# Six tiles of split weights that begin at six different places of a 64 byte line, in a two-layer hybrid mixer block

## The chip, the cores and the metric

One core of a Trainium2 chip runs the whole program in one launch. The metric is the device time of that launch in microseconds (us). A core has five engines that run side by side: TensorE (PE in the profile, with its loads of weights as a row of their own, PEld), VectorE (DVE), ScalarE (ACT), GpSimd (POOL) and SyncE (SP), which issues the transfers from main memory.

## The reference

Two layers of a block that mixes four branches: retention with a decay in both directions, a short gated convolution of 3 taps, a convolution of 31 taps with a layer norm, and windowed attention with grouped keys. Each layer has a stream x of 512 tokens and a context stream of 256 tokens, both 1024 wide; in the second layer the context gives only keys, values and states.

```python
hx = modulate(rmsnorm(x, norm_w[l]), shift_x[:, None], scale_x[:, None])
px = split_proj(hx @ w_in[l])                 # 1024 -> 11008 columns
...
merged = sum(jax.nn.sigmoid(g) * (br @ w_branch[i]) for i, (g, br) in enumerate(...))
out = merged @ w_out
x = x + gate_x[:, None] * out_x
```

Everything is float32. What matters here is that nearly all of the arithmetic is `activations @ weights`, with weights that are used once per stream.

## The kernel before, in words

**Products.** Activations lie transposed, 128 features on the partitions and the tokens along a row: 512 columns for x, 256 for the context. A product runs in the type float32r, and to keep precision each operand is split in two parts, a high part (h) and a low part (l). `mm3` (L478) makes three matmuls for each of the eight blocks of 128 features: (weight h, x h), (weight h, x l), (weight l, x h). The weight block of 128x128 is what is loaded into the array, the activations stream through it, so every matmul comes with a load of its own and a tile of weights, 128x1024, gives 24 matmuls.

**Split weights.** A tile of raw weights comes by a transfer into one of two tiles `w0`, `w1` (or, while the context stream is worked on, into two rows of 512 columns). `w_split` (L445) then makes the two parts: ScalarE copies the raw weights into `wh` (which rounds them to float32r), VectorE subtracts that from the raw weights and writes `wl`. The parts go to the next of three pairs of tiles, `self.wt` (L292): wh0 and wl0, wh1 and wl1, wh2 and wl2, taken in turn by `take("wt")` (L448). `w_ahead` (L461) splits up to two tiles of weights ahead of the one in use, so ScalarE writes into a pair as soon as the matmuls of the tile three before it are done. The branch weights `w_b` (L450 to L454) and the activations are split into rows of another pool and don't use these six tiles.

**Other loads into the array.** The attention and retention products load blocks of rows; transposes load 128 columns of a row or of a probability tile `p`; the modulation (L559) loads four columns of a small tile `s4` at a time: `self.s4[:, 2 * h + k]` (L568), eight places that lie 16 bytes apart, against activations of 256 columns.

**Order.** TensorE's order is written by hand; side work (attention, retention, convolutions, norms) is woven between the matmuls of the projections by `slot` (L337), by estimates of when each engine is free. None of these estimates looks at an address. The order of the streams is context of layer 0, x of layer 0, keys and values of the context in layer 1, x of layer 1, and the last projection in two halves of 256 columns (L1267).

**Where tiles lie.** The pool `cp` (L290) lays its tiles one behind the other: `w0`, `w1`, the six tiles of split weights, six tiles `p` for attention, constants, vectors, and small tiles. A tile of 1024 float32 is 4096 bytes of each partition, 64 lines of 64 bytes.

**The convolution of 31 taps** (L878) is a row of VectorE instructions `y[a:b] += w * u[a+d:b+d]` with d from -15 to 15: for a negative d the write begins -d elements into its row, for a positive d the read begins d elements into its row.

Of the kernel before, what the change touches and what calls it, by code (L numbers as in the profile page):

```python
# [9 lines left out]
F32R = mybir.dt.float32r  # L10
# [15 lines left out]
P = 128  # L26
# [97 lines left out]
class Row:  # L124
# [3 lines left out]
    def __init__(self, free, ring, tile, w, parts):  # L128
        self.free, self.ring = free, ring
        self.r = tile[:, :w] if parts else None  # L130
        self.a = tile[:, :w].bitcast(F32) if parts else tile[:, :w]
# [146 lines left out]
class Block:  # L278
    def __init__(self, ctx, tc, xc, vec, cst, w_a, w_g, w_b, w_o, w_m, out):
        self.tc, self.nc = tc, Tally(tc.nc)  # L280
        self.xc, self.out = xc, out
        self.wsrc = {"a": w_a, "g": w_g, "b": w_b, "o": w_o}
        self.w_m = w_m

        rp = ctx.enter_context(tc.tile_pool(name="rp", bufs=1))
        rp.tile([P, PAD], F32, name="fill")
        self.arena = Arena(rp, NROWS, 12)
        self.arena.relief = self.relief

        self.cp = cp = ctx.enter_context(tc.tile_pool(name="cp", bufs=1))  # L290
        self.wraw = [cp.tile([P, 1024], F32, name=f"w{i}") for i in range(2)]
        self.wt = [[cp.tile([P, 1024], F32R, name=f"w{p}{i}") for p in "hl"] for i in range(3)]  # L292
        self.pt = [cp.tile([P, 640], F32, name=f"p{i}") for i in range(6)]
        pp = ctx.enter_context(tc.tile_pool(name="pp", bufs=1, space=PSUM))
        nc = self.nc
        self.cst = cp.tile([P, NC_], F32, name="cst")
        self.vec = cp.tile([P, NV], F32, name="vec")
        nc.sync.dma_start(self.vec, vec)
        nc.sync.dma_start(self.cst[:, :NCE], cst[:, :NCE])
        self.late_consts = lambda: nc.sync.dma_start(self.cst[:, NCE:], cst[:, NCE:])  # L300
        self.rings = {}
        self.dense = [pp.tile([P, 512], F32, name=f"d{i}") for i in range(3)]
        self.ovs = [pp.tile([P, 512], F32, name="ov")]
        self.work = [pp.tile([P, 512], F32, name=f"k{i}") for i in range(4)]
        self.turn = {}
        self.wq, self.wraws, self.wready, self.wkeep = [], [], {}, {}
        self.lanes = [[] for _ in range(5)]
        self.turns = 0
        self.flow = None
# [1161 lines left out]
```

## Time and profile before

| | us |
|---|---|
| median of 3 runs | 1832.24 (1830.57 to 1833.15) |
| the profiled execution, its own time | 1832.62 |
| its span, first to last instruction | 1830.5 |
| TensorE matmul busy in it | 1799.5 |
| VectorE busy | 1329.4 |
| ScalarE busy | 847.1 |

The span is shorter than the execution's own time by 2.1 us, which lies around the first and the last instruction. A matmul's bar in the trace is longer than its share of the time, because matmuls overlap: from one to the next only the distance of their starts counts. TensorE is busy in all but 31 us of the span, most of those at the start and at the end.

### The profile page before, as it was taken

The numbers are of one execution on the slowest core, as the hardware profiler recorded it, in microseconds if no ns is written. First come the engines' busy times: TensorE is split into PE (matmuls) and PEld (weight loads), VectorE is DVE, ScalarE is ACT, GpSimd is POOL, SyncE is SP. The second block draws the span as 40 slices with busy tenths as digits, with TensorE's granted clock in tenths as the row PEclk, the third lists the DMA queues.
The fourth block names the chain that finished last, engine by engine and source line by source line (L and its number), as shares of the span: only waits on it lengthen the run. The fifth ranks groups of instructions, "written<-read, shape, count | busy, mean of one in ns | idle before, by whom it ended". The sixth has DMA issues, their size and how long they took to land. (4 is left out here: it accounts for less than half of the span.)

```text
span 1830.5 us, 27546 instructions
## 1 busy us (share of the span) xinstructions
PE 1799.5 (98%) x10224; PEld 1562.1 (85%) x10224; DVE 1329.4 (73%) x2643; ACT 847.1 (46%) x1616; POOL 27.9 (2%) x34
## 2 busy tenths in 40 slices
PE   6999999999999999999999999999999999999997
PEld 4999999998888888788888889888888888888887
DVE  8899999884556669996898457447999865444445
ACT  6666765553554544423423336445534554323232
POOL 1000000000000000000000000000000000000000
PEclk8999999999999999999999999999999999999999
DMA  8736377743122222233555552322122222332233
GB/s 306 252 125 213 111 242 231 235 138 116 69 70 67 84 81 83 91 108 124 185 170 168 169 182 75 116 70 70 66 91 87 80 98 87 115 104 87 87 117 114
DMA packets 104646, 232.60 MB, mean 127 GB/s; under 512 B 12864, under 2 KB 20800, under 8 KB 104512
## 3 DMA queue, kind: packets, MB, share of 16 engines
q1 hardware_dynamic: 104512, 230.84, 37.9%
q8 instruction: 80, 1.31, 0.3%
q14 instruction: 54, 0.44, 0.1%
HBM read 218.73 MB, written 5.24 MB: 122 GB/s over the span
## 5 line engine op out<-in xcount | busy, mean ns | idle before, releaser
L187 PE MATMUL d<-r,wh 128*128 128x512 f32 (+1 forms) x3136 | 942.7, 383 | 0.3 <-DVE r L187 0.3
L187 PEld LDWEIGHTS d<-r,wh 128*128 128x128 f32 x3136 | 572.7, 188 | 106.2 <-DVE r L187 0.5
L187 PE MATMUL d<-r,wl 128*128 128x512 f32 (+1 forms) x1568 | 597.6, 381 | 0.0
L187 DVE TENSOR_TENSOR wl<-w,wh 128x1024 fp32r<-128x1024 f32 x193 | 235.6, 1221 | 233.8 <-ACT wh L187 229.0
L187 ACT ACTIVATE wh<-w 128x1024 fp32r<-128x1024 f32 x193 | 205.0, 1062 | 411.5 <-PE d L187 358.2
L187 PEld LDWEIGHTS d<-r,wl 128*128 128x128 f32 x1568 | 294.8, 188 | 57.6
L187 ACT ACTIVATE r<-r 128x512 fp32r<-128x512 f32 (+3 forms) x264 | 150.5, 588 | 211.6 <-DVE r L187 94.5
L187 DVE TENSOR_TENSOR r<-r,r 128x512 fp32r<-128x512 f32 (+5 forms) x338 | 207.8, 629 | 35.2 <-ACT r L187 31.2
L187 DVE SCALAR_TENSOR_TENSOR r<-r,h_cfw,r 128x503 f32<-128x503 f32 (+19 forms) x360 | 229.1, 648 | 2.0
L187 PE MATMUL d<-r,r 128*128 128x512 f32 x768 | 184.8, 389 | 0.5 <-DVE r L187 0.5
L187 ACT ACTIVATE wh<-r 128x512 fp32r<-128x512 f32 x208 | 129.2, 631 | 101.7 <-PE d L187 88.5
L187 PEld LDWEIGHTS d<-r,r 128*128 128x128 f32 x768 | 144.1, 188 | 30.8 <-DVE r L187 0.9
L187 DVE TENSOR_TENSOR wl<-r,wh 128x512 fp32r<-128x512 f32 x208 | 140.6, 685 | 18.6 <-ACT wh L187 17.5
L187 DVE SCALAR_TENSOR_TENSOR r<-r,d 128x512 f32<-128x512 f32 (+1 forms) x156 | 92.7, 594 | 56.4 <-PE d L187 32.4
L187 ACT ACTIVATE r<-d 128x512 f32<-128x512 f32 (+2 forms) x234 | 118.5, 507 | 14.1 <-PE d L187 9.5
L187 PE MATMUL k<-r,r 128*128 128x128 f32 (+2 forms) x752 | 112.3, 290 | 2.7 <-ACT p L187 2.6
L187 ACT ACTIVATE r<-k 128x512 fp32r<-128x512 f32 (+4 forms) x162 | 76.9, 522 | 70.5 <-PE k L187 69.2
L187 PEld LDWEIGHTS k<-r,r 128*128 128x128 f32 x752 | 99.5, 191 | 8.9 <-ACT p L187 6.2
L187 ACT ACTIVATE p<-k,s_nm 128x256 f32<-128x256 f32 (+1 forms) x144 | 69.7, 497 | 78.0 <-DVE s_nm L187 77.9
L187 DVE SCALAR_TENSOR_TENSOR r<-r,cs,r 128x256 f32<-128x256 f32 x196 | 83.6, 477 | 2.0 <-DMA r<-w_m 1.4
L187 DVE TENSOR_TENSOR r<-k,r 128x512 fp32r<-128x512 f32 (+2 forms) x88 | 54.4, 651 | 9.5 <-ACT r L187 9.3
L187 ACT ACTIVATE p<-p,s_rc 128x512 f32<-128x512 f32 (+2 forms) x80 | 51.3, 719 | 9.6 <-DVE s_rc L187 9.6
(393 smaller groups left out, 2245.3 us busy)
## 6 DMA issues: line engine op xcount, KB each, us to landing
w<-w_a SPq DMA_DIRECT2D x108, 512.0 KB, 3.5
r<-w_a SPq DMA_DIRECT2D x128, 256.0 KB, 5.0
w<-w_g SPq DMA_DIRECT2D x64, 512.0 KB, 3.5
r<-w_m SPq DMA_DIRECT2D x96, 256.0 KB, 3.8
r<-w_b SPq DMA_DIRECT2D x96, 256.0 KB, 3.4
r<-w_g SPq DMA_DIRECT2D x64, 256.0 KB, 3.8
w<-w_o SPq DMA_DIRECT2D x21, 512.0 KB, 3.5
r<-xc SPq DMA_DIRECT2D x24, 256.0 KB, 3.8
```

Source lines behind the costliest of these rows:

```text
L187: return f(*a, **k)
```

## The change

The six tiles become 1040 columns wide (4160 bytes, 65 lines of 64 bytes) and each is used through a view of 1024 columns that begins 0, 4, 2, 12, 8 or 6 elements in, which is 0, 16, 8, 48, 32 or 24 bytes.

```diff
         self.wraw = [cp.tile([P, 1024], F32, name=f"w{i}") for i in range(2)]
-        self.wt = [[cp.tile([P, 1024], F32R, name=f"w{p}{i}") for p in "hl"] for i in range(3)]
+
+        self.wt = [[cp.tile([P, 1040], F32R, name=f"w{p}{i}")[:, o:o + 1024] for p, o in zip("hl", os)]
+                   for i, os in enumerate(((0, 4), (2, 12), (8, 6)))]
```

| tile | wh0 | wl0 | wh1 | wl1 | wh2 | wl2 |
|---|---|---|---|---|---|---|
| view begins at byte | 0 | 16 | 8 | 48 | 32 | 24 |

All who use the six tiles (`w_split`, `mm3`) take slices of the view, with the same widths as before. The raw tiles, the rows and their pool stay where they are; what lies behind the six tiles in the pool moves up by 384 bytes, six whole lines.

## Rows read from the trace of the kernel before

**Rows 1.** The page, part 1: busy us (share of the span) and instructions.

```profile
PE 1799.5 (98%) x10224; PEld 1562.1 (85%) x10224; DVE 1329.4 (73%) x2643; ACT 847.1 (46%) x1616; POOL 27.9 (2%) x34
```

**Rows 2.** Stretches: from:to, sum; busy PE, PEld, DVE, ACT, POOL; clock, DMA, GB/s.

```profile
100.00:300.00 200.00, 200.00 (x1669) 199.25 (x1667) 190.51 (x462) 128.09 (x294) 5.25 (x6) 1.00 0.57 183
...
400.00:900.00 500.00, 497.55 (x2477) 416.08 (x2476) 361.18 (x677) 223.94 (x419) 7.48 (x9) 1.00 0.29 97
...
1160.00:1760.00 600.00, 597.12 (x2905) 497.99 (x2904) 382.16 (x664) 251.72 (x457) 6.74 (x8) 1.00 0.27 90
```

**Rows 3.** Waits: who for whom, us in total, times, longest; PE, PEld, ACT.

```profile
PE d L187 <- DVE wl L187: 0.6, 1, 0.6
...
PEld d L187 <- DVE wl L187: 0.8, 1, 0.8
...
ACT wh L187 <- PE d L187: 446.7, 233, 6.6
```

**Rows 4.** Timeline, PE, x stream: start, us, instruction.

```profile
1699.92 0.39 PE L187 MATMUL d<-r,wl 128*128 128x512 f32 x1
...
1700.60 0.39 PE L187 MATMUL d<-r,wl 128*128 128x512 f32 x1
...
1701.28 0.39 PE L187 MATMUL d<-r,wl 128*128 128x512 f32 x1
```

**Rows 5.** Timeline, PE, context stream.

```profile
200.25 0.28 PE L187 MATMUL d<-r95l,wh 128*128 128x256 f32 x1
200.37 0.28 PE L187 MATMUL d<-r95h,wl 128*128 128x256 f32 x1
200.49 0.28 PE L187 MATMUL d<-r109h,wh 128*128 128x256 f32 x1
```

**Rows 6.** Timeline, PEld, the same stretch.

```profile
200.25 0.19 PEld L187 LDWEIGHTS d<-r95h,wl 128*128 128x128 f32 x1
200.37 0.19 PEld L187 LDWEIGHTS d<-r109h,wh 128*128 128x128 f32 x1
```

**Rows 7.** Timeline, PEld, seven loads for transposes, merged.

```profile
1437.32 0.79 PEld L187 LDWEIGHTS k<-cst,p 128*128 128x128 f32 x7
```

**Rows 8.** Groups by shape, PE: count | busy us, mean ns | idle before.

```profile
L187 PE MATMUL d<-r,wh 128*128 128x512 f32 x2880 | 896.0, 392 | 0.0
L187 PE MATMUL d<-r,wl 128*128 128x512 f32 x1440 | 561.3, 390 | 0.0
...
L187 PE MATMUL d<-r,wh 128*128 128x256 f32 x256 | 46.7, 284 | 0.3 <-DVE r L187 0.3
...
L187 PE MATMUL d<-r,wl 128*128 128x256 f32 x128 | 36.2, 283 | 0.0
...
L187 PE MATMUL d<-r109l,wh 128*128 128x256 f32 x86 | 24.3, 283 | 0.0
```

**Rows 9.** Groups by shape, ACT: the writes of wh.

```profile
L187 ACT ACTIVATE wh<-w 128x1024 fp32r<-128x1024 f32 x193 | 205.0, 1062 | 411.5 <-PE d L187 358.2 <-issue 39.9 <-DMA w<-w_o 5.7
L187 ACT ACTIVATE wh<-r 128x512 fp32r<-128x512 f32 x208 | 129.2, 631 | 101.7 <-PE d L187 88.5 <-issue 2.7 <-ACT r L187 2.6
```

**Rows 10.** Groups by shape, DVE: the writes of wl, the taps, one aligned form.

```profile
L187 DVE TENSOR_TENSOR wl<-w,wh 128x1024 fp32r<-128x1024 f32 x193 | 235.6, 1221 | 233.8 <-ACT wh L187 229.0 <-PE k L187 3.5 <-PE ov L187 0.9
L187 DVE TENSOR_TENSOR wl<-r,wh 128x512 fp32r<-128x512 f32 x208 | 140.6, 685 | 18.6 <-ACT wh L187 17.5
...
L187 DVE SCALAR_TENSOR_TENSOR r<-r,h_cfw,r 128x511 f32<-128x511 f32 x16 | 11.9, 745 | 0.1
...
L187 DVE SCALAR_TENSOR_TENSOR r<-r,h_cfw,r 128x504 f32<-128x504 f32 x16 | 11.8, 738 | 0.2
...
L187 DVE SCALAR_TENSOR_TENSOR r<-r,h_cfw,r 128x497 f32<-128x497 f32 x16 | 11.7, 730 | 0.1
...
L187 DVE SCALAR_TENSOR_TENSOR r<-r,mod,r 128x512 f32<-128x512 f32 x16 | 11.4, 746 | 0.8 <-ACT r L187 0.8
```

**Rows 11.** Timeline, PEld, thirteen loads of four columns of s4, merged.

```profile
37.59 1.45 PEld L187 LDWEIGHTS k<-r,s 128*4 128x4 f32 x13
```

**Rows 12.** One stretch, instructions on wh alone: sum; busy PE, PEld, DVE, ACT.

```profile
100.00:300.00 200.00, 153.52 (x838) 130.12 (x836) 71.90 (x107) 65.15 (x105) 1.00 0.57 183
```

## The prediction, made before the result was known

> **What bounds the kernel now.** I read the page's first part, then the busy time by stretch, the waits, the timeline and the groups by shape. The first shows TensorE busy 98% of the span, VectorE 73%, ScalarE 46% [rows 1]. [...] The waits show that the split weights are never what TensorE lacks: in the whole run its matmuls of projections wait once for a written wl, 0.6 us, its loads once, 0.8 us; the other way round ScalarE waits 446.7 us, 233 times, until the matmuls have let a wh go [rows 3]. So the writes of the six tiles lie off the path, and the path is the distance from one matmul's start to the next.
>
> That distance is read from the timeline. With 512 columns three matmuls begin every 0.68 us (1699.92, 1700.60, 1701.28), so 227 ns each [rows 4]; with 256 columns they begin every 0.12 us [rows 5], and the load of each block begins with the matmul before it, 0.12 us ahead of its own [rows 6]. What the loads alone could do is seen where the matmul is short: seven loads for transposes of 128 columns take 0.79 us, the last one's bar about 0.14, so they begin (0.79 - 0.14)/6 = 108 ns apart [rows 7]. A load of 128 columns thus needs about 108 ns of the array's load path. It is covered by a matmul of 512 columns with 227 - 108 = 119 ns to spare and by one of 256 columns with 120 - 108 = 12 ns to spare.
>
> **The change part by part.** It adds and removes no instruction, no byte and no wait; each instruction keeps its width. Three things are touched.
>
> *Loads from the six tiles.* By the groups there are 2880 + 1440 = 4320 matmuls of 512 columns on them [rows 8]. Those of 256 columns are split into many groups by the names of the rows: 256 + 128 in the last projection, 24 groups of 86 in the context stream of layer 0 such as the one shown, and 432 in smaller groups, 2880 in all [rows 8]. The count of writes agrees: 193 whole and 208/2 half-wise written tiles are 297 [rows 9], times 24 is 7128, plus 72 for the three tiles that the last projection's second half uses again, is 7200. At 227 and 120 ns these are 981 + 346 = 1327 us of the span. What a load costs from a place that is no multiple of 16 bytes the trace doesn't show, since blocks of a tile, of a row and of `p` begin 512 bytes apart. The nearest row is `s4`: thirteen loads, 16 bytes from one place to the next, 1.45 us, so (1.45 - 0.09)/12 = 113 ns apart without a long one among them, at every one of the four sixteenth-byte places of a line [rows 11]. Its loads are only four columns wide, so this bounds the price of the start, not that of a long run across lines. For the low end I take no gain, except as the rival below; for the high end a load that takes twice its 108 ns. I take 0: the start costs nothing at 16, 32 and 48 bytes, and what a start at 8 or 24 adds has to pass 12 ns (11% of a load) before the first matmul begins later, 119 ns before one of 512 columns does. Sum: 0 us.
>
> *Writes of the six tiles.* ScalarE writes wh in 1062 ns (1024 columns) or 631 ns (512), so (1062 - 631)/512 = 0.84 ns a column [rows 9]; VectorE reads wh and writes wl in 1221 or 685 ns, 1.05 ns a column [rows 10]. For VectorE the trace shows shifted starts: the taps of the 31 tap convolution read or write from 4 to 60 bytes into a row, and their time is a straight line, 745 ns at 511 columns, 738 at 504, 730 at 497, beside 746 at 512 columns that begin on a line [rows 10]. A start anywhere costs VectorE nothing. For ScalarE no row shows it; I bound it by 0 and by a doubled write. In the tightest stretch the instructions on wh take it 65.15 of its 128.09 us busy in 200 [rows 12, 2]; one pair of three begins its wh off a multiple of 16 bytes, so doubling those adds 22 us, to 150 of 200, still idle a quarter of the time, with two tiles split ahead of use. I take 0. If the cover were gone, each late tile would cost TensorE at most the added 0.63 or 1.06 us. Nothing below 0 can come of a faster write, since TensorE waits 0.6 and 0.8 us for them in all [rows 3].
>
> *What moves up behind them.* The six tiles grow by 64 bytes each, one whole line, so `p`, the constants and the small tiles keep their place in a line. 0 us.
>
> So the sum is 0 on the profiled execution's 1832.62 us, which lies 0.4 us above the median of the runs; I predict the median, 1832.2. A measurement of this kernel can tell a change from none at about 0.2%, 3.7 us.
>
> **The rivals.**
>
> *Slower: loads that cut a line uncover themselves in the matmuls of 256 columns.* The place is the context stream and the last projection, where a load has 12 ns to spare; it decides from there on. If only starts that are no multiple of 16 bytes suffer, these are wh1 and wl2, three of the nine loads of a turn of the ring, 2880/3 = 960 matmuls. A load half as long again, 162 ns, begins each of them 162 - 120 = 42 ns later: 40 us, 1873. A doubled load, 216 ns, gives 96 x 960 = 92 us, 1924, and still hides under 512 columns. If all starts but 0 suffered, seven of nine, 2240 matmuls, the half would cost 94 us, 1926. For it: no row shows a long load at such a place. Against it: the small loads at 16 byte steps are alike [rows 11], and a shift of the start leaves the number of bytes the same, so that a load of 512 bytes would have to pay far more than for one piece of a line more. [...] Chance 0.09.
>
> *Faster: the shift parts two streams that disturb each other.* With 256 columns a load of four columns leaves 113 ns between matmuls [rows 11] and one of 128 columns 120 [rows 5], so a full load may cost the matmul beside it about 7 ns. Should that be both streams meeting in the same part of a line, and should the five shifted tiles (seven of nine loads) be rid of it, 7200 x 7/9 = 5600 matmuls gain 7 ns, 39 us: 1793. Against it: the four columns of `s4` pass all four 16 byte places beside the same kind of stream and the distance doesn't move. Chance 0.05.
>
> *The change doesn't only do what it says.* Views instead of tiles might make the program's dependences coarser, so that a load waits for both halves of a tile written half-wise, or change the order on VectorE and ScalarE. The half-wise tiles are 104 [rows 9]; if each made TensorE wait for one more VectorE write, 0.685 us, that is 71 us, 1903; with two tiles ahead it would be a small part of them, some us either way. Chance 0.04.
>
> **How the numbers follow.** No effect has the chance 0.82, the three rivals 0.09, 0.05 and 0.04. The range is that of no effect, 0.2% to either side, 1828.6 to 1835.9: the others lie far outside and together stay under 2 in 10. Faster takes 0.05 and a little of the last case, 0.06; slower takes 0.09, the rest of the last case and a drift past the bound, 0.12.
>
> **What would show it.** Right: 27546 instructions in the same order; the loads d<-r,wh and d<-r,wl at the same mean; starts 0.12 and 0.227 us apart in the same stretches; the writes of wh and wl still at 1062 and 1221 ns. Wrong: three of nine matmuls in the context stream further apart than 120 ns while those of 512 columns keep 227 (the slower rival, and its share tells which starts suffer); distances under 120 or 227 (the faster one); new waits of PE for wl (the third). A longer wh or wl alone, with TensorE's distances unchanged, would correct the second part and leave the time.

## The result and the profile after

The changed kernel takes 1846.8 us (median of 4 runs, 1845.1 to 1849.9), the kernel before 1832.6: ratio 1.0081, 95% interval 1.0064 to 1.0099. It is slower by 0.8%; I had forecast no effect.

The page of the changed kernel, span and first part:

```profile
span 1845.0 us, 27546 instructions
...
PE 1815.1 (98%) x10224; PEld 1558.4 (84%) x10224; DVE 1330.1 (72%) x2643; ACT 847.1 (46%) x1616; POOL 27.9 (2%) x34
```

The same instructions, VectorE and ScalarE as busy as before, TensorE busy 15.6 us longer [rows 1]. The span grew by 14.5 us, so the whole loss is TensorE's. What it waited for hasn't changed. The waits of the changed kernel, TensorE's matmuls and loads for written weights (who for whom, us in total, times, longest):

```profile
PE d L187 <- DVE wl L187: 0.8, 1, 0.8
...
PEld d L187 <- DVE wl L187: 1.0, 1, 1.0
```

Each is still one wait [rows 3]. The writes of the six tiles, groups by shape:

```profile
L187 ACT ACTIVATE wh<-w 128x1024 fp32r<-128x1024 f32 x193 | 205.1, 1063 | 426.9 <-PE d L187 367.5 <-issue 42.2 <-DMA w<-w_o 8.8
L187 ACT ACTIVATE wh<-r 128x512 fp32r<-128x512 f32 x208 | 129.1, 632 | 95.2 <-PE d L187 83.8 <-ACT r L187 2.5 <-ACT wh L187 2.2
...
L187 DVE TENSOR_TENSOR wl<-w,wh 128x1024 fp32r<-128x1024 f32 x193 | 235.9, 1223 | 244.5 <-ACT wh L187 238.1 <-PE k L187 4.5 <-PE ov L187 1.4
L187 DVE TENSOR_TENSOR wl<-r,wh 128x512 fp32r<-128x512 f32 x208 | 140.8, 686 | 16.9 <-ACT wh L187 15.5
```

1063, 632, 1223 and 686 ns beside 1062, 631, 1221 and 685 [rows 9, 10]: a shifted start cost neither ScalarE nor VectorE anything here.

What is left is the distance between matmuls. The cleanest row for it is one piece of the chain that ended last: 1080 matmuls in the x stream of layer 1 that follow each other without a wait, 30 times 24 on the six tiles and 12 on rows. Of the kernel before (start, us, what):

```profile
1526.90 244.83 PE d L187 x1080
```

and of the changed kernel:

```profile
1538.03 249.26 PE d L187 x1080
```

244.83/1080 is 226.7 ns. Of the 4.43 us more, 4.1 fall on the 720 matmuls of the six tiles, 5.7 ns each. The granted clock is 1.00 in both kernels from 1530 to 1770 us, so it isn't the clock. It goes the other way where the matmuls are 256 columns wide. The context stream of the changed kernel, one tile of weights from its first matmul to the next work, on the timeline:

```profile
200.49 0.28 PE L187 MATMUL d<-r51h,wh 128*128 128x256 f32 x1
...
203.22 0.28 PE L187 MATMUL d<-r135h,wl 128*128 128x256 f32 x1
203.34 0.38 PE L187 MATMUL k<-cst,p 128*128 128x128 f32 x2
```

24 matmuls in 2.85 us are 119 ns each, where before they were 120 [rows 5]; other tiles come to 116 or 118. Between 100 and 300 us the windows show 12 matmuls more than before done [rows 2]:

```profile
100.00:300.00 200.00, 199.88 (x1681) 198.72 (x1680) 192.06 (x468) 128.68 (x295) 5.26 (x6) 1.00 0.58 186
```

Added up over both traces, from each matmul's start to the next one's, by the program's own order of matmuls: the 4320 of 512 columns on the six tiles went from 994.0 to 1013.2 us, the 2880 of 256 columns from 354.0 to 349.8, and everything else took 0.5 less. That is 19.2 - 4.2 - 0.5 = 14.5 us, the growth of the span.

### The profile page after: what moved, and what is told of

It is laid out like the page before. It is cut to its first block, busy times and chain, and to the rows that moved or that the text cites. A ratio compares the mean times of both kernels' runs of the same rounds, so it can differ in the third digit from the quotient of the medians.

```text
span 1845.0 us, 27546 instructions
## 1 busy us (share of the span) xinstructions
PE 1815.1 (98%) x10224; PEld 1558.4 (84%) x10224; DVE 1330.1 (72%) x2643; ACT 847.1 (46%) x1616; POOL 27.9 (2%) x34
## 5 line engine op out<-in xcount | busy, mean ns | idle before, releaser
L187 PE MATMUL d<-r,wh 128*128 128x512 f32 (+1 forms) x3136 | 955.1, 387 | 0.3 <-DVE r L187 0.3
L187 PE MATMUL d<-r,wl 128*128 128x512 f32 (+1 forms) x1568 | 604.6, 386 | 0.0
L187 DVE TENSOR_TENSOR wl<-w,wh 128x1024 fp32r<-128x1024 f32 x193 | 235.9, 1223 | 244.5 <-ACT wh L187 238.1
L187 ACT ACTIVATE wh<-w 128x1024 fp32r<-128x1024 f32 x193 | 205.1, 1063 | 426.9 <-PE d L187 367.5
```

Source lines behind the costliest of these rows:

```text
L187: return f(*a, **k)
```

## The experiments

Ratios below are to runs of the kernel before on the same chip, with a 95% interval. The row after each is the chain's piece of 1080 matmuls in that run.

**Matmuls alone, first try** (`m1_places`). A kernel that computes nothing of the reference: `mm3`'s instruction alone, 24 times in a case, with load and stream at chosen places. The tiles are `wa` to `wp` and `xa` to `xp`, so `wh` in its rows is the eighth tile and no high part.

```diff
+    def case(n, wo, xo, reps=24):
+        p = ps[turn[0] % 3][:, :n]
...
+        for j in range(reps):
+            i = j // 3
+            nc.tensor.matmul(p, ws[wo[j % len(wo)]][:, cs(i % 8)], xs[xo[j % len(xo)]][:, :n], start=j == 0, stop=j == reps - 1)
```

> A kernel that computes nothing of the reference: TensorE alone, after its operands are written once, streams 24 matmuls per case with 512, 256, 384 and 128 columns; first the load begins at 0, 4, ... 60 bytes of a line with the stream at 0, then the stream at 4 ... 60 with the load at 0, then both at the same place, then the three pairs of the change in the order h, h, l. Theory A (a load and the stream that runs beside it collide by where they lie to each other): with both at one place 227 ns (512) and 120 ns (256) everywhere; with the load shifted alone 229 to 237 ns at 512 and 113 to 119 at 256, and much the same with the stream shifted alone. Theory B (a load pays for its own place, whatever the stream's): the load's shift alone counts, so both at one place is as dear as the load alone, and the stream alone shifted stays at 227 and 120. Theory C (the writes of ScalarE and VectorE into the six tiles disturb the loads): no such writes run here, so 227 and 120 in all cases.

With 512 columns and load and stream both at the first place a matmul takes 226.6 ns; for the other loads 226.7 to 235. With the order h, h, l of the change's three pairs it is 232.3, 233.3 and 232.2 ns. No other engine runs here, so the loss needs none, and theory C falls. In the 233 ns cases all loads come from one tile at one place: six places that differ from one another aren't needed for it. With 128 columns nothing moves, and there I take the load to set the pace: at the 0.42 ns a column of `m2_grid` below, 128 columns of the stream are 53 ns, an estimate, and a matmul took 112. Timeline, 24 matmuls a row, three places of the load:

```profile
768.51 2.84 PE L1440 MATMUL d<-xa,wh 128*128 128x128 f32 x24
771.20 2.84 PE L1440 MATMUL d<-xa,wi 128*128 128x128 f32 x24
773.88 2.84 PE L1440 MATMUL d<-xa,wj 128*128 128x128 f32 x24
```

Rows begin 2.68 to 2.69 us apart, 112 ns a matmul; all 16 places came to 111.6 or 111.7. **At 128 columns a load costs the same from every place, 112 ns**, and what changes at 512 columns is how a load and the stream beside it get along. Theory B, that a load pays for its own place, falls with it, and with the stream shifted alone: by theory B 227 ns throughout, measured 226.6 to 240.0. One flaw: the tiles of this kernel were 1040 columns wide too, so its places ran 68 and not 4 bytes apart. And with load and stream shifted alike it gave 227 to 238 ns, which the strict form of theory A, in which only their difference counts, doesn't allow.

**All six at 32 bytes** (`all32`): `((8, 8), (8, 8), (8, 8))` for the pairs of starts.

> All six tiles begin 32 bytes into a line, so that they lie alike among themselves and differ from the rows that stream. Theory A: the matmuls of 512 columns begin 231 to 235 ns apart (232.7 ns from wh2 to wh2 in the changed kernel), 4320 x 4 to 8 ns = 17 to 35 us, those of 256 columns 1 to 2 ns closer, 3 to 6 us back: 1844 to 1862. Theory D (what counts is that the six places differ from one another): 1832.6, 227 and 120 ns. Theory B: as theory A or, if a place that is a multiple of 16 bytes is free, 1832.6.

1847.8 us, ratio 1.0091 (1.0076 to 1.0106).

```profile
1539.36 249.71 PE d L187 x1080
```

Six starts alike are as slow as six different ones. That would speak against theory D, but the tiles are still 1040 columns wide, so in memory the six don't lie alike and the growth is in this run too. What theory D falls by is `m1_places`, where one place alone took 233 ns.

**Everything at 32 bytes** (`move32`): `PAD = 488` for 480, the fill ahead of the rows.

> The kernel before with the fill ahead of its rows 32 bytes longer, so that rows, split weights and all behind them begin 32 bytes into a line together. Theory A: nothing changes, 1832.6 within 0.2%, 227 and 120 ns. Theory B: as all32.

1831.3 us, ratio 1.0001 (0.9991 to 1.0010).

```profile
1526.15 244.86 PE d L187 x1080
```

With rows and split weights moved together by 32 bytes nothing changes. Beside `all32` it doesn't isolate the place of the rows, since the width of the six tiles differs too. The runs of matmuls alone do: a load 32 bytes from its stream modulo 256 (its ninth place) took 233.4 ns in `m1_places`, and in `m3_clean` below 233.2 alone and 227.4 with the stream moved along. What counts is **where the load lies to the stream**.

**The two halves of the change** (`xonly`, `ctxonly`): `w_split` takes the shifted views for one kind of tile and views at 0 for the other; the tiles stay 1040 wide.

```diff
-        parts = [self.take("wt")]
+        narrow = key[3] or (key[0] == "o" and key[1] == DEPTH - 1)
+        os = (0, 0) if narrow else ((0, 4), (2, 12), (8, 6))[self.turn.get("wt", 0) % 3]
+        parts = [[x[:, o:o + 1024] for x, o in zip(self.take("wt"), os)]]
```

> The six shifted starts only while tiles of 512 column matmuls are split; for those of the context stream and of the last projection (256 columns) the views begin at 0. Theory A with the accounts of the two traces (4320 matmuls of 512 columns +19 us, 2880 of 256 columns -4 us): 1831 + 19 to 20 = 1850 to 1852, slower than the whole change. If the whole loss came in the context stream, where VectorE is busiest: 1831.

1844.7 us, 1.0073 (1.0059 to 1.0086).

```profile
1536.91 249.25 PE d L187 x1080
```

> The other half of the change: shifted starts only for the tiles of 256 column matmuls. Theory A: 1831 - 4 = 1827, starts 116 to 120 ns apart there, 227 with 512 columns. If the loss came in the context stream: 1845.

1844.9 us, 1.0076 (1.0063 to 1.0089).

```profile
1536.32 248.96 PE d L187 x1080
```

Both missed, and the second is the one to look at: its tiles for 512 columns begin on a line, at byte 0 of it, and the 1080 matmuls are as slow as with shifted starts. Only the growth of the tiles is left to do that: 64 bytes each put them at 0, 64, 128, 192, 256 and 320 bytes from where they were. By tile, the mean distance from a matmul on wh to the next one on it was 229.0 ns for wh0 (at 0), 235.3 for wh1 (at 128) and 229.0 for wh2 (at 256). 0 and 256 alike, 128 not: theory G, that a load's place relative to the stream counts within 256 bytes. `xonly` missed by the same cause: at 64 byte steps its 256 column matmuls kept more of the gain (347.3 us against 354.0) than I had credited.

**40 bytes for the narrow matmuls** (`ctx40`): as above with `os = (10, 10) if narrow else (0, 0)`.

> Tiles of 256 column matmuls begin 40 bytes into a line, high and low part alike, tiles of 512 column matmuls at 0. Theory A with the kernel of matmuls alone, where a load at 40 beside a stream at 0 came to 113.6 ns: 2880 x (120 - 113.6) = 18 us less, 1813, if the matmuls fall into that rhythm here too; if they stay at the mean of the other shifted starts, 117 to 119 ns: 1822 to 1828. If places don't matter in the whole kernel's traffic: 1831.

1846.5 us, 1.0077 (1.0063 to 1.0090). A miss: the 512 column matmuls paid for the grown tiles as in `ctxonly`, and the 256 column ones came to 351.7 us, 2.3 less than before, since the place called 40 in `m1_places` was ten steps of 68 bytes, 680, which is 168 within 256; a true 40 took 119.3 ns in `m3_clean` below.

**All pairs of places** (`m2_grid`), still on tiles of 1040 columns.

> Matmuls alone again. [...] Then all 16 x 16 places of load and stream in steps of 4 bytes: theory A in its strict form (only the difference of the two places counts) wants equal values along a difference; m1 already showed 227 to 238 ns with both at one place, so I expect that the strict form fails and that values repeat when both move by 32 bytes (4 and 36, 20 and 52 were alike); at 512 columns no pair under 226, at 256 some at 113.

At 512 columns the pairs gave 226.6 to 240.0 ns, none under 226.6; at 256 columns 113.3 to 123.5. Values don't follow the difference of the places alone: at one difference of 0 they still run from 226.6 to 237.6. Where the stream itself begins counts too: averaged over the sixteen loads, a stream 68 bytes on took 236.3 ns and one 252 bytes on 228.4. Narrower loads at the first place took 226.6, 230.1, 230.1 and 231.8 ns for 128, 96, 64 and 32 columns beside 512. (From 256 to 512 columns a settled matmul at the first place grows from 120.0 to 226.6 ns, 0.42 ns a column; 512 of them are 213 ns, an estimate from these two, which leaves 13 ns of the 226.6.) A stream that gives way to the load column by column would make the 13 ns smaller with a narrower load, a fixed price of a change of weights would leave them at 13: they grew to 19. Neither of these two simple pictures holds.

**The growth alone** (`wide0`): tiles of 1040 columns, all views at 0.

> The change without its shifted starts: six tiles of 1040 columns, each view beginning at 0, so every view begins on a line of 64 bytes, at 0, 64, 128, 192, 256 and 320 bytes beside the place it had. Theory G (what counts is where the load lies to the stream within some 256 bytes: in the run with shifted starts for the context only, the tiles at 256 and 320 gave the same distances as those at 0 and 64, those at 128 and 192 others): 512 columns as there, 229 to 235 ns, and 256 columns as in the run with shifted starts for x only, 115 to 118 ns: 1832 + 17 - 7 = 1842, with the small parts 1840 to 1846. Theory L (the place within a line of 64 bytes counts): 1832.

1843.0 us, 1.0062 (1.0047 to 1.0077).

```profile
1533.57 248.96 PE d L187 x1080
```

**The starts alone** (`line1088`): tiles of 1088 columns, 4352 = 17 x 256 bytes, with the change's six starts.

> Tiles of 1088 columns with the six starts of the change, 0, 16, 8, 48, 32, 24 bytes: the shift within the line alone, without the 64 bytes by which each tile moved its followers. Theory G: still slower, by the places 0 to 48 of 256: 512 columns 229 to 236 ns, 1840 to 1850. If only the growth of the tiles counted: 1832.

1841.6 us, 1.0056 (1.0041 to 1.0071).

```profile
1534.29 247.34 PE d L187 x1080
```

**Neither** (`wide1088`): tiles of 1088 columns, views at 0.

> Tiles of 1088 columns (4352 bytes, 17 times 256), views at 0. Theory G: every load lies to its stream as before, modulo 256: 1832, 227 and 120 ns. If the period is longer than 256 bytes, or if what counts is what moves behind the six tiles: 1840 or more.

1830.7 us, 0.9996 (0.9987 to 1.0006).

```profile
1525.20 244.83 PE d L187 x1080
```

The three settle it. Each of the change's two parts costs 10 to 12 us by itself, together 14 or 15, and a growth by a multiple of 256 bytes, which moves what lies behind it four times as far, costs nothing. Theory L falls with `wide0`. A rival by which the things behind the tiles count, and the more the further they move, falls with `wide1088`. By where they lie within 256 bytes they could still count, since there they moved by six times 256. But in `wide0` all matmuls that don't use the six tiles took 469.1 us, as before, and the 1080 matmuls, whose operands all lie ahead of these things, carry the loss themselves.

**Matmuls alone on clean places** (`m3_clean`): one tile of weights and one of activations, both from a multiple of 256 bytes.

> Matmuls alone, with one tile of weights and one of activations that both begin at a multiple of 256 bytes, so that places aren't mixed with those of the tiles as in the two runs before. Load at 0 to 252 bytes in steps of 4 beside a stream at 0, with 512 and 256 columns, then at 256 and 512, then both shifted alike by steps of 16; then 256 columns with the order h, h, l at all pairs of steps of 16. Theory G: 226.7 and 120 ns at 0, 256 and 512; between them 228 to 240 at 512 columns, 113 to 123 at 256; both shifted alike by a multiple of 32 as at 0.

Timeline, 24 matmuls a row, 512 columns; the load at 0, 16, 256 and 512 bytes, the stream at 0:

```profile
41.08 5.61 PE L1434 MATMUL da<-x,w 128*128 128x512 f32 x24
...
63.16 5.76 PE L1434 MATMUL db<-x,w 128*128 128x512 f32 x24
...
397.38 5.62 PE L1434 MATMUL db<-x,w 128*128 128x512 f32 x24
402.84 5.60 PE L1434 MATMUL dc<-x,w 128*128 128x512 f32 x24
```

The next rows begin at 46.53, 68.76, 402.84 and 408.28, so 227.1, 233.3, 227.5 and 226.7 ns a matmul, with the few in which the rhythm settles; settled, 226.7, 233.4, 226.6 and 226.6. Of the 64 places within 256 bytes 8 gave 226.6 or 226.7, the rest 228 to 238. But a pair of places doesn't always settle alike: in `m1_places`, `m2_grid` and here, with the stream at its first place, a load 204 bytes on took 234.1, 226.6 and 226.6 ns, one 252 bytes on 226.7, 233.4 and 226.6. Load and stream both at the first place gave 226.6 or 226.7 in all three. With 256 columns, the load at 0 and at 64 bytes, each with the row behind it:

```profile
496.30 3.03 PE L1434 MATMUL db<-x,w 128*128 128x256 f32 x24
499.17 3.00 PE L1434 MATMUL dc<-x,w 128*128 128x256 f32 x24
...
541.70 2.89 PE L1434 MATMUL dc<-x,w 128*128 128x256 f32 x24
544.43 3.01 PE L1434 MATMUL da<-x,w 128*128 128x256 f32 x24
```

2.87/24 = 119.6 ns against 2.73/24 = 113.8 (settled 120.0 in the kernel before and 113.4 here). Moved together by odd multiples of 16 bytes, load and stream took 230.1 ns, by multiples of 32 227.4: so here too the stream's own place has some part. The orders h, h, l with 256 columns came to 113.3 to 123.9 ns; high and low part both at 64 bytes gave 113.3.

**A version that beats both** (`best64`): tiles of 1088 columns, views at 0 for the wide matmuls, at 64 bytes for the narrow ones.

```diff
+        os = (16, 16) if narrow else (0, 0)
```

> Tiles of 1088 columns, so that all lie alike modulo 256 bytes; for matmuls of 512 columns the views begin at 0, for those of 256 columns at 64 bytes, high and low part alike, the place that gave 113.3 ns in the run of matmuls alone. Theory G: 512 columns stay at 227 ns; at 256 columns 2880 x (120 - 113.3) = 19 us less on TensorE, 1812. What may take some of it back: VectorE is busy 95% of the middle of the context stream, so TensorE at 113/120 would catch up with it there: up to 1822. If the rhythm of the matmuls alone isn't reached between other work, 117 to 119 ns and 1822 to 1829.

1823.9 us, ratio to the kernel before 0.9961 (0.9948 to 0.9975).

```profile
1520.55 244.86 PE d L187 x1080
```

and in its windows

```profile
100.00:300.00 200.00, 199.71 (x1688) 197.91 (x1687) 193.56 (x471) 128.09 (x294) 5.25 (x6) 1.00 0.58 189
```

The wide matmuls keep 227 ns, and 19 matmuls more than before get done in those 200 us [rows 2]. The gain is 7 us and not the 19 of the rhythm alone: the narrow matmuls came to 116.3 ns on average, a third of them at 113 or 114 and most others at 117 to 119. TensorE was busy 199.71 of the 200 us, so VectorE didn't hold it up. From 200 to 240 us one tile of weights runs at 113 and 114 ns from its first block to its last and another, at the same places, at 117 to 119: what decides which I didn't find.

## Why the prediction was wrong

- **The bound was right**: TensorE's distances, 227 and 120 ns, set the time, and nearly all of the change in time is in them.
- **The writes were right**: ScalarE, which no row had shown, wrote at 8 and 32 bytes in the same time as at 0; VectorE as its taps had said.
- **The load's own time was a little off**: 108 ns came from transposes; loads of split weights took 112 in `m1_places`, so 8 ns were to spare beside 256 columns, not 12. That decided nothing.
- **The step that failed is the price of the loads: "I take 0", with "what a start at 8 or 24 adds has to pass 12 ns (11% of a load) before the first matmul begins later, 119 ns before one of 512 columns does".** It took a load as work that lies hidden beside the stream as long as it ends in time. Where it could be measured alone a load's time never changed (112 ns from every place), and the bars of the loads from wh have a mean of 188 ns before and after, so nothing says that a margin was used up. A load lengthened or shortened the matmul beside it, and the loss came where I had 119 ns to spare. The measured term is 19 us on the wide matmuls and -4 us on the narrow ones.
- **The term "the small tiles keep their place in a line. 0 us" failed the same way.** I asked what the growth of 64 bytes does to the place in a line and to the tiles behind the six, not what it does to the six among themselves. `wide0` puts it at 11.6 us. The views were not the only change in the diff: the width was one too. And the line of 64 bytes in which I counted is no boundary that any run showed: at 64, 128 and 192 bytes `m3_clean` took 233.2, 233.5 and 228.9 ns, for 226.7 at 0.
- **The slower rival was the wrong one**: it put the loss on the narrow matmuls and let the wide ones hide everything. The wide ones lost 19 us, the narrow ones gained 4. Nor was a start that is no multiple of 16 bytes what counted: in `wide0` every view begins at a multiple of 64, and it lost 11.6 us.
- **The faster rival had half of the mechanism**, load and stream that disturb each other by their places, and the sign for the narrow matmuls: -4 us of the 39 it allowed. It took meeting at one place for the dear case; beside 512 columns that was the cheap one, 226.6 or 226.7 ns. I ruled it to 0.05 on the `s4` loads [rows 11]. They were four columns wide, and the 113 ns that they kept from place to place say nothing of a load of 128; I wrote that they bound "the start, not that of a long run", and then used them as if they bounded both. The even 226 or 227 ns of the trace before couldn't warn of it: in that kernel every block of the six tiles and every row that streams beside it begins at a multiple of 256 bytes.

What stays open is how load and stream come to disturb each other. The 13 ns that were left of the 226.6 don't shrink with narrower loads, 0, 256 and 512 bytes are alike (226.6 or 226.7 ns in `m3_clean`), the distance varies from one matmul to the next (226 to 239 ns on the tile of weights that begins at 1604.33 us of the changed kernel), and the same pair of places doesn't always settle alike; why a place that is dear beside 512 columns can be cheap beside 256 (64 bytes in `m3_clean`: 233.2 ns for 226.7, and 113.4 for 120) I didn't settle.

## What to carry to other kernels

Where TensorE is the bound and each matmul brings its own load, as here, look at the addresses of weights and activations to each other: they moved a matmul of 512 columns by up to 6%, 226.6 to 240.0 ns in `m2_grid`. Keep both at multiples of 256 bytes for 512 columns, which was fast in every run that had it (226.6 or 226.7 ns in the kernel before, `wide1088`, `best64` and `m3_clean`), and let a tile grow only by such multiples (1830.7 us in `wide1088`, 1843.0 in `wide0`). For narrower matmuls try other places, one run of matmuls alone shows them, and count on less than it shows: 64 bytes gave 113.4 ns in `m3_clean` and 116.3 in `best64`. When a diff gives a tile another width, ask what that does to the addresses of its neighbours before asking what the slices do.

## What the runs showed of the hardware that I had not expected

- The distance of matmuls with a load each depends on the place of the load relative to the stream, and in part on the stream's own: 226.6 to 240 ns with 512 float32r columns, 113.3 to 123.5 with 256. A load 0, 256 or 512 bytes from the stream took the same, 226.6 or 226.7 ns, one 128 bytes from it 233.5 (`m3_clean`), and no pair settled under 226.6.
- Matmuls of 128 columns, whose loads came from 16 places in turn, all took 112 ns a piece: no place was better for the load itself.
- A step that looks harmless, six tiles each wider by exactly 64 bytes, cost 0.6% of the whole kernel (`wide0`).
